# Five groups of blocks by seven products, woven over all steps of a feed-forward part, with wider splits

## The chip, the core and the metric

The kernel runs on one core of a Trainium2 chip. The metric is the device time of one execution in microseconds. Five engines work side by side, each through its own queue of instructions in a fixed order: TensorE (PE in the rows; its weight loads are PEld), VectorE (DVE), ScalarE (ACT), GpSimd (POOL) and SyncE (SP, which issues the loads). Data lies in SBUF, matmul results in eight banks of PSUM.

## What is computed

One decoder layer on 256 tokens in fp32, width 2048: a half-weighted SwiGLU, a mixer (gated linear recurrence and short convolution), a second half-weighted SwiGLU, a gated per-layer input, and a final norm. Cut to what matters here:

```
def swiglu(x, w_gate, w_up, w_down):
    return (jax.nn.silu(x @ w_gate) * (x @ w_up)) @ w_down

h = h + 0.5 * swiglu(rms_norm(h, norm_ffn1), ffn1_gate, ffn1_up, ffn1_down)
u = rms_norm(h, norm_mix); proj = u @ w_in
...                                            # mixer, added to h
h = h + 0.5 * swiglu(rms_norm(h, norm_ffn2), ffn2_gate, ffn2_up, ffn2_down)
h = h + sigmoid(rms_norm(h, norm_ple) @ w_ple_gate) * (p @ w_ple)
y = rms_norm(h, norm_final)
```

Gate and up are 2048 x 5632, that is 44 blocks of 128 columns; down is 5632 x 2048.

## The kernel before

**Splits.** Precision comes from writing each fp32 number as a high and a low part. The unit of work is a step: one weight tile (`raw`, 128 x 16 blocks x 128, 1 MB) is loaded by SP; ACT copies it to the high part (`hi`, L97), DVE subtracts to get the low part (`lo`, L98), and PE forms the product of the 16 blocks with the activations `xs` (high and low side by side, 512 columns): per block one matmul of 512 columns with `hi` (L120) and one of 256 with `lo` (L119, L122), all into one PSUM bank `ps`. A step of 12 or 8 blocks works alike. Before, `hi` and `lo` are half tiles of 8 blocks (four buffers each), so a step has two copies and two subtractions.

**The feed-forward part** goes in chunks of 8, 12, 12 and 12 blocks of the 44: gate and up steps for the chunk (gate: product, scale by the row norm `rb` L153, sigmoid, multiply L375; up: scale, multiply L381, split to `hid` L162 and L163), then 16 down steps, one for each block of the model's width, which multiply `hid` by 8 or 12 blocks and add half the result to `hT` (ACT L206, DVE L207, then L208 which frees the bank).

**Seven products.** In each chunk of 12 the first four blocks of gate and up are a group computed another way: blocks are paired to 2 x 2 (two halves of the tokens, two halves of the 2048 inputs, and gate and up as columns) and seven products of sums take the place of eight. A group has eight parts kp. Each has a half a (three products, nine matmuls of 512 columns, L293 to L295) and a half b (four products, twelve matmuls). The weights come as `sraw`; the sums are `st` (L320 to L322, the last written back into `sraw`); ACT copies and DVE subtracts (L309, L310) give `ahi`, `alo`, `bhi`, `blo`, one buffer each. The activations' sums `xf` are made once per feed-forward part by `forms`, sent to memory by POOL and loaded again for each kp. A group keeps seven of the eight banks from its first matmul to its last. Then `epi` combines them on DVE, and `turn` transposes the result by PE (L392) into `hid`. Before, the halves of a group stand one after each gate or up step of their chunk; the down steps have none.

**Order.** `steps` is one list. Step i loads step i + 3, splits step i + 2, and multiplies itself; a scheduler then places the instructions on each engine by when it expects them to be ready, and that order is fixed.

Of the kernel before, what the change touches and what calls it, by code (L numbers as in the profile page):

```python
# [7 lines left out]
F32 = mybir.dt.float32  # L8
# [24 lines left out]
CHUNKS = ((8, 0), (12, 4), (12, 4), (12, 4))  # L33
NS = 4
NK2 = NB // 2

RAW_BUFS = 3
LOAD_AHEAD = 3
# [13 lines left out]
def kernel(  # L52
# [26 lines left out]
    def tt(shape=(P, T), dtype=F32, tag="t", bufs=6):  # L79
        return tmp.tile(list(shape), dtype, tag=tag, name=tag, bufs=bufs)  # L80
# [13 lines left out]
    def split_piece(s, a, b):  # L94
        hi, lo = s.parts[a // s.half]
        r, sl = s.raw[:, a:b, :], slice(a % s.half, a % s.half + b - a)
        A.activation(hi[:, sl, :], r, AF.Copy)  # L97
        V.tensor_tensor(lo[:, sl, :], r, hi[:, sl, :].bitcast(F32), ALU.subtract)  # L98
# [31 lines left out]
    def weights(s, k):  # L130
        hi, lo = s.parts[k // s.half]
        return hi[:, k % s.half, :], lo[:, k % s.half, :]
# [23 lines left out]
    def sig(src):  # L156
        s = tt(tag="s", bufs=3)
        A.activation(s, src, AF.Sigmoid)
        return s
# [63 lines left out]
    def at(i, f):  # L223
        steps[i].hooks.append(f)
# [17 lines left out]
    FA, FB = ("P1", "P2", "P6"), ("P5", "P3", "P7", "P4")  # L242
    FORMS = {"P4": 0, "P5": 1, "P6": 2, "P7": 3, "P3": 4}
# [9 lines left out]
    def forms(kp, c_gain, sd):  # L253
        pool = st["spool"]
        a = pool.tile([P, 5, P], F32, tag="ec", name="fa", bufs=2)
        f = pool.tile([P, 5, P], F32, tag="ey", name="ff", bufs=2)
# [5 lines left out]
        a11, a21, a12 = a[:, 0, :], a[:, 1, :], a[:, 2, :]  # L262
        V.tensor_tensor(a21, a21, rho, ALU.mult)
        V.tensor_tensor(f[:, 0, :], a[:, 3, :], rho, ALU.mult)
        V.tensor_tensor(f[:, 1, :], a21, f[:, 0, :], ALU.subtract)
        V.tensor_tensor(f[:, 2, :], f[:, 1, :], a11, ALU.subtract)
        V.tensor_tensor(f[:, 3, :], a11, a21, ALU.subtract)
        V.tensor_tensor(f[:, 4, :], a12, f[:, 2, :], ALU.add)
        A.activation(x[:, 0], f, AF.Copy)
        V.tensor_tensor(x[:, 1], f, x[:, 0].bitcast(F32), ALU.subtract)  # L270
        nc.gpsimd.dma_start(sd[:, kp, :], x.rearrange("p a f t -> p (a f t)").bitcast(F32))

    def seven(ws, sd, finish):
# [24 lines left out]
        def ld(kp):  # L298
            def f(s):
                pool = st["spool"]  # L300
                r = g["raw", kp] = pool.tile([P, 4, T2], F32, tag="sraw", name="sraw", bufs=1)
                nc.sync.dma_start(r, ws[kp])
                x = g["xf", kp] = pool.tile([P, 10 * P], F32, tag="xf", name="xf", bufs=2)
                nc.sync.dma_start(x, sd[:, kp, :])
            return f

        def pieces(hi, lo, todo):
            for sl, src in todo:
                A.activation(hi[:, sl, :], src, AF.Copy)  # L309
                V.tensor_tensor(lo[:, sl, :], src, hi[:, sl, :].bitcast(F32), ALU.subtract)  # L310

        def sp_a(kp):
            def f(s):
                pool, r = st["spool"], g["raw", kp]
                t = g["t", kp] = pool.tile([P, 3, T2], F32, tag="st", name="st", bufs=1)
                hi, lo = g["a", kp] = tuple(pool.tile([P, 3, T2], F32R, tag="a" + n, name="a" + n, bufs=1)
                                            for n in ("hi", "lo"))
                pieces(hi, lo, [(slice(0, 2), r[:, 0:2, :])])

                V.tensor_tensor(t[:, 0:2, :], r[:, 0:3:2, :], r[:, 3:4, :].broadcast_to([P, 2, T2]), ALU.add)  # L320
                V.tensor_tensor(t[:, 2, :], t[:, 0, :], r[:, 2, :], ALU.add)
                V.tensor_tensor(r[:, 3, :], t[:, 2, :], r[:, 1, :], ALU.add)  # L322
                pieces(hi, lo, [(2, t[:, 2, :])])
            return f

        def sp_b(kp):
            def f(s):
                pool, r, t = st["spool"], g["raw", kp], g["t", kp]
                hi, lo = g["b", kp] = tuple(pool.tile([P, 4, T2], F32R, tag="b" + n, name="b" + n, bufs=1)
                                            for n in ("hi", "lo"))  # L330

                pieces(hi, lo, [(slice(0, 3, 2), t[:, 0:2, :]), (slice(1, 4, 2), r[:, 2:4, :])])
            return f

        def epi(s):
            pool = st["spool"]

            def e(tag, bufs=2):
                return pool.tile([P, 5 * P], F32, tag=tag, name=tag, bufs=bufs)[:, :T2]

            def silu_mul(c, u):
                y = e("ey")
# [4 lines left out]
            a, c0, v = e("ea", 1), e("ec"), e("ey")  # L347
# [7 lines left out]
            c1 = e("ec")  # L355
# [11 lines left out]
        return res  # L367

    def ffn(wg, wu, wsd, wd, c_gain, c_next, name):
# [15 lines left out]
        def turn(k0, c):  # L385

            for k in range(0, NS, 2):
                ps = new_ps()
                for i in range(2):
                    for w in range(2):  # L390
                        o = i * T + w * P
                        TE.transpose(ps[:, o:o + P], c[w][:, (k + i) * P:(k + i + 1) * P], ident)  # L392
                d = st["hid"][:, k0 + k:k0 + k + 2, :]
                p = ps.rearrange("p (k t) -> p k t", k=2)
                A.activation(d[:, :, :T], p, AF.Copy)
                V.tensor_tensor(d[:, :, T:], p, d[:, :, :T].bitcast(F32), ALU.subtract)

        i0 = len(steps)
        f0 = ng = 0
        for ci, (nf, ns) in enumerate(CHUNKS):  # L400
            last = ci == len(CHUNKS) - 1
            std = []
            for k in range(ns, nf):
                std.append(Step(wg[f0 + k], NB, *gemm_in(g_epi)))
                std.append(Step(wu[f0 + k], NB, *gemm_in(u_epi(k))))
            if ns:
                got = []
                h = seven(wsd[ng], sd, lambda *c, got=got: got.extend(c))
                ng += 1
                seq, std = [*h[:2]], std  # L410
                for x in h[2:]:
                    seq += [std.pop(0), x]
                seq += std
                seq[-1].hooks.append(lambda got=got: turn(0, got))
                steps.extend(seq)
            else:
                steps.extend(std)
            order = [*range(ns, nf), *range(ns)]
            for j in range(NB):
# [11 lines left out]
                add(wd[j][:, f0:f0 + nf, :], nf, mm, epi)  # L431
            f0 += nf
        at(i0 + 5, rows)
# [16 lines left out]
    def mixer():  # L450
# [31 lines left out]
        def i_mm(kc):  # L482
            def mm(s):
                if kc == 0:
                    st["iv"] = new_ps(), new_ps()
                for k in range(4):
                    hi, lo = (t[:, 4 * (k % 2):4 * (k % 2) + 4, :].rearrange("p a c -> p (a c)")
                              for t in s.parts[k // 2])
# [165 lines left out]
        def norm_rows(key, g):  # L654
            d = m["m1"].tile([P, T], F32R, tag="nr", name="nr", bufs=4)
# [276 lines left out]
    n = len(steps)  # L932
    for i, s in enumerate(steps):
        if 0 < i < n - LOAD_AHEAD:
            load(steps[i + LOAD_AHEAD])
# [105 lines left out]
```

## Time and profile before

| | us |
|---|---|
| median of 3 runs (2029.29 to 2030.66) | 2030.2 |
| profiled execution | 2028.77 |
| its span | 2027.0 |
| PE busy (99% of the span) | 2002.1 |
| PE's weight loads busy (85%) | 1731.7 |
| DVE busy (81%) | 1636.0 |
| ACT busy (55%) | 1117.1 |

The profile's span runs from the first instruction to the last; the execution around it is 1.8 us longer. The first feed-forward part lies at 0 to 741 us, the mixer to 1181, the second feed-forward part to 1909, the per-layer input after it. An engine's busy time says how much work it has; whether a wait matters is seen only from what the engine that ends last, PE here, was waiting for in that stretch. The rows below show both for the stretches that the change touches.

### The profile page before, as it was taken

The numbers are of one execution on the slowest core, as the hardware profiler recorded it, in microseconds if no ns is written. First come the engines' busy times: TensorE is split into PE (matmuls) and PEld (weight loads), VectorE is DVE, ScalarE is ACT, GpSimd is POOL, SyncE is SP. The second block draws the span as 40 slices with busy tenths as digits, with TensorE's granted clock in tenths as the row PEclk, the third lists the DMA queues.
The fourth block names the chain that finished last, engine by engine and source line by source line (L and its number), as shares of the span: only waits on it lengthen the run. The fifth ranks groups of instructions, "written<-read, shape, count | busy, mean of one in ns | idle before, by whom it ended". The sixth has DMA issues, their size and how long they took to land.

```text
span 2027.0 us, 28859 instructions
## 1 busy us (share of the span) xinstructions
PE 2002.1 (99%) x11094; PEld 1731.7 (85%) x11094; DVE 1636.0 (81%) x2645; ACT 1117.1 (55%) x1716; POOL 11.6 (1%) x23
## 2 busy tenths in 40 slices
PE   8999999999999999999999999999999999999997
PEld 7888888888888888888888888888888888888886
DVE  8988886888688775689798789788968886887886
ACT  7655555555555554553566556455555555555663
POOL 0000000000000000000000000000000000000000
PEclk9999999999999999999999999999999999999998
DMA  8686666665665465544355567766666666654742
GB/s 293 211 277 242 233 205 216 219 237 200 222 232 198 156 212 187 189 166 146 129 184 187 187 227 274 226 232 226 208 208 224 232 202 220 228 202 153 249 164 84
DMA packets 69546, 419.93 MB, mean 207 GB/s; under 512 B 7712, under 2 KB 7968, under 8 KB 35744
## 3 DMA queue, kind: packets, MB, share of 16 engines
q1 hardware_dynamic: 67104, 407.60, 59.0%
q0 software_dynamic: 2304, 10.49, 1.3%
q8 instruction: 87, 1.43, 0.3%
q14 instruction: 51, 0.42, 0.1%
HBM read 405.48 MB, written 12.58 MB: 206 GB/s over the span
## 4 chain that ended last, share of the span: by engine, by line
PE 89%; DVE 4%; DMA 4%; issue 1%; ACT 1%; SPq 0%; DVEq 0%; ACTq 0%
PE ps L120 49%; PE ps L119 23%; PE ps L294 3%; PE ps L295 3%; PE ps L293 3%; PE ps L122 2%; DVE lo L98 2%; DMA sraw<-w1s 1%; DMA raw<-w1d 1%; DMA raw<-w1u 1%; PE ps L591 1%; PE ps L494 1%; PE ps L493 1%; PE ps L492 1%; DMA sraw<-w2s 1%
## 5 line engine op out<-in xcount | busy, mean ns | idle before, releaser
L120 PE MATMUL ps<-xs,hi 128*128 128x512 f32 x3056 | 1082.8, 395 | 9.5 <-DVE xs L167 6.1
L98 DVE TENSOR_TENSOR lo<-raw,hi 128x1024 fp32r<-128x1024 f32 (+2 forms) x660 | 751.1, 1139 | 239.3 <-ACT hi L97 235.7
L97 ACT ACTIVATE hi<-raw 128x1024 fp32r<-128x1024 f32 (+2 forms) x660 | 652.7, 990 | 516.6 <-PE ps L120 323.6
L119 PE MATMUL ps<-xs,lo 128*128 128x256 f32 x2865 | 801.5, 280 | 0.4 <-DVE lo L98 0.2
L120 PEld LDWEIGHTS ps<-xs,hi 128*128 128x128 f32 x3056 | 569.7, 188 | 137.5 <-ACT hi L97 7.2
L119 PEld LDWEIGHTS ps<-xs,lo 128*128 128x128 f32 x2865 | 538.0, 188 | 10.4 <-DVE lo L98 1.8
L120 PE MATMUL ps<-hid,hi 128*128 128x512 f32 x1384 | 477.6, 394 | 0.0
L119 PE MATMUL ps<-hid,lo 128*128 128x256 f32 x1258 | 354.4, 283 | 0.5 <-ACT hid L162 0.5
L120 PEld LDWEIGHTS ps<-hid,hi 128*128 128x128 f32 x1384 | 251.5, 188 | 48.8
L119 PEld LDWEIGHTS ps<-hid,lo 128*128 128x128 f32 x1258 | 236.2, 188 | 7.3 <-ACT hid L162 1.3
L309 ACT ACTIVATE ahi<-sraw 128x1024 fp32r<-128x1024 f32 x48 | 51.0, 1063 | 125.2 <-DMA sraw<-w1s 61.5
L146 ACT ACTIVATE t<-ps 128x256 f32<-128x256 f32 x191 | 70.2, 372 | 88.3 <-PE ps L120 88.3
L320 DVE TENSOR_TENSOR st<-sraw 128x1024 f32<-128x1024 f32 x48 | 58.8, 1224 | 69.2 <-DMA sraw<-w1s 38.7
L147 DVE TENSOR_TENSOR t<-ps,t 128x256 f32<-128x256 f32 x191 | 80.3, 421 | 24.0 <-ACT t L146 23.9
L120 PE MATMUL ps<-mixout,hi 128*128 128x512 f32 x240 | 83.6, 397 | 0.0
L153 DVE TENSOR_TENSOR t<-t,rb 128x256 f32<-128x256 f32 x183 | 76.9, 422 | 2.7
L293 PE MATMUL ps<-bhi,xf 128*128 128x512 f32 x192 | 74.9, 390 | 0.0
L295 PE MATMUL ps<-blo,xf 128*128 128x512 f32 x192 | 74.9, 390 | 0.0
L294 PE MATMUL ps<-bhi,xf 128*128 128x512 f32 x192 | 74.9, 390 | 0.0
L208 DVE SCALAR_TENSOR_TENSOR hT<-ps,t 128x256 f32<-128x256 f32 x141 | 59.7, 424 | 13.7 <-DVE t L207 1.4
L207 DVE TENSOR_TENSOR t<-hT,t 128x256 f32<-128x256 f32 x141 | 59.1, 420 | 10.6 <-ACT t L206 10.6
L206 ACT ACTIVATE t<-ps 128x256 f32<-128x256 f32 x141 | 51.9, 369 | 27.5 <-PE ps L120 27.5
(234 smaller groups left out, 2078.7 us busy)
## 6 DMA issues: line engine op xcount, KB each, us to landing
raw<-w_in SPq DMA_DIRECT2D x48, 1024.0 KB, 4.8
raw<-w1d SPq DMA_DIRECT2D x48, 768.0 KB, 4.2
raw<-w2d SPq DMA_DIRECT2D x48, 768.0 KB, 4.3
raw<-w2g SPq DMA_DIRECT2D x32, 1024.0 KB, 4.9
raw<-w2u SPq DMA_DIRECT2D x32, 1024.0 KB, 5.1
raw<-w1u SPq DMA_DIRECT2D x31, 1024.0 KB, 5.3
raw<-w1g SPq DMA_DIRECT2D x30, 1024.0 KB, 5.0
xf<-forms SPq DMA_DIRECT2D x48, 640.0 KB, 4.0
```

The source lines that it names most:

```text
L97: A.activation(hi[:, sl, :], r, AF.Copy)
L98: V.tensor_tensor(lo[:, sl, :], r, hi[:, sl, :].bitcast(F32), ALU.subtract)
L119: TE.matmul(ps[:, T:], lo, m[:, :T], start=False, stop=False)
L120: TE.matmul(ps, hi, m, start=first, stop=last)
L146: A.activation(t, ps[:, T:], AF.Copy)
L147: V.tensor_tensor(t, ps[:, :T], t, ALU.add)
L153: V.tensor_tensor(dst, t, rb, ALU.mult)
L207: V.tensor_tensor(t, hT[:, j, :], t, ALU.add)
L208: V.scalar_tensor_tensor(hT[:, j, :], ps[:, :T], c, t, ALU.mult, ALU.add)
L293: TE.matmul(g[p], x_lo, hi[:, i, :], start=kp == 0, stop=False)
L294: TE.matmul(g[p], x_hi, hi[:, i, :], start=False, stop=False)
L295: TE.matmul(g[p], x_hi, lo[:, i, :], start=False, stop=kp == NK2 - 1)
```

## The change

- `CHUNKS` now names groups per chunk: 0, 1, 2 and 2, five for each feed-forward part in place of three. 20 of 44 blocks go by seven products, 12 before.
- `weave` orders a feed-forward part: after 14 gate and up steps, half steps of the groups, in one stream, stand after the other steps in the ratio of 4/3 per full step, down steps included; half steps left over at a chunk's end follow at once. A group's transposes are steps of their own, at least two steps after its end. No half step stands within 1.5 steps after a group's end.
- `hi` and `lo` of a step are whole tiles in two buffers. ACT still copies in two halves, DVE subtracts once.
- Half a is split in one operation on each engine (1536 columns), half b in one of 2048. All four sums are in `st`, and `raw` buffers, four of them, serve both kinds of steps; loads run four steps ahead.
- `forms` makes four sums, and the fifth is taken as it is. Some buffers of small tiles are fewer.

```diff
-CHUNKS = ((8, 0), (12, 4), (12, 4), (12, 4))
+CHUNKS = ((8, 0), (12, 1), (12, 2), (12, 2))
+LEAD = 14
+HALVES = 4 / 3
-RAW_BUFS = 3
-LOAD_AHEAD = 3
+RAW_BUFS = 4
+LOAD_AHEAD = 4
...
     def new_parts(s):
-        s.half = s.nk // 2 if s.nk > 8 else s.nk
-        s.parts = [tuple(wpool.tile([P, NB // 2, P], F32R, tag=t, name=t) for t in ("hi", "lo"))
-                   for _ in range(s.nk // s.half)]
+        s.parts = tuple(wpool.tile([P, NB, P], F32R, tag=t, name=t, bufs=2) for t in ("hi", "lo"))
...
         new_parts(s)
-        for k0 in range(0, s.nk, s.half):
-            split_piece(s, k0, k0 + s.half)
+        hi, lo = s.parts
+        h = s.nk // 2
+        for a in (0, h):
+            A.activation(hi[:, a:a + h, :], s.raw[:, a:a + h, :], AF.Copy)
+        V.tensor_tensor(lo[:, :s.nk, :], s.raw[:, :s.nk, :], hi[:, :s.nk, :].bitcast(F32), ALU.subtract)
...
+        def parts(key, kp, n, src):
+            hi, lo = g[key, kp] = tuple(st["spool"].tile([P, n, T2], F32R, tag=key + t, name=key + t, bufs=1)
+                                        for t in ("hi", "lo"))
+            A.activation(hi, src, AF.Copy)
+            V.tensor_tensor(lo, src, hi.bitcast(F32), ALU.subtract)
...
+                r = g["raw", kp]
+                parts("a", kp, 3, r[:, 0:3, :])
+                t = g["t", kp] = st["spool"].tile([P, 4, T2], F32, tag="st", name="st", bufs=1)
                 V.tensor_tensor(t[:, 0:2, :], r[:, 0:3:2, :], r[:, 3:4, :].broadcast_to([P, 2, T2]), ALU.add)
                 V.tensor_tensor(t[:, 2, :], t[:, 0, :], r[:, 2, :], ALU.add)
-                V.tensor_tensor(r[:, 3, :], t[:, 2, :], r[:, 1, :], ALU.add)
-                pieces(hi, lo, [(2, t[:, 2, :])])
+                V.tensor_tensor(t[:, 3, :], t[:, 2, :], r[:, 1, :], ALU.add)
...
         def sp_b(kp):
-            def f(s):
-                pool, r, t = st["spool"], g["raw", kp], g["t", kp]
-                hi, lo = g["b", kp] = tuple(pool.tile([P, 4, T2], F32R, tag="b" + n, name="b" + n, bufs=1)
-                                            for n in ("hi", "lo"))
-
-                pieces(hi, lo, [(slice(0, 3, 2), t[:, 0:2, :]), (slice(1, 4, 2), r[:, 2:4, :])])
-            return f
+            return lambda s: parts("b", kp, 4, g["t", kp])
...
+        def other(x, ci):
+            w = x.nk / NB
+            steps.append(x)
+            state["n"] += 1
+            state["rest"] -= w
+            for t in turns:
+                t[1] += w
+            if state["n"] < LEAD:
+                return
+            state["credit"] += w * HALVES
+            while halves and state["credit"] >= 1 and state["rest"] <= 0:
+                half()
+                state["credit"] -= 1
+            state["credit"] = min(state["credit"], 2.0)
+            if ci is not None:
+                turn_all(ci, 2.0)
+
+        for ci, (std, down) in enumerate(others):
+            for x in std:
+                other(x, ci)
+            while halves and groups[halves[0][0]][2] <= ci:
+                half()
+            turn_all(ci, 0.0)
+            for x in down:
+                other(x, None)
```

The order of the instructions shows what this does on the engines. In the new kernel the lines are L117 for `lo`, L315 for `alo` and `blo`, L322 to L324 for `st`, L210 and L211 for a down step's sum, L122, L123 and L125 for its matmuls.

DVE where half steps stood in the kernel before, between gate and up steps:

```order
L321 TENSOR_TENSOR st_3861<-st_3861,sraw_3807 128x512
L98 TENSOR_TENSOR lo_3884<-raw_3859,hi_3883 128x1024
L147 TENSOR_TENSOR t_3852<-ps_3819,t_3852 128x256
L322 TENSOR_TENSOR sraw_3807<-st_3861,sraw_3807 128x512
L153 TENSOR_TENSOR t_3852<-t_3852,rb_76 128x256
L310 TENSOR_TENSOR alo_3863<-st_3861,ahi_3862 128x512
L381 TENSOR_TENSOR t_3852<-t_3852,t_3783 128x256
L98 TENSOR_TENSOR lo_3886<-raw_3859,hi_3885 128x1024
L163 TENSOR_TENSOR hid_303<-t_3852,hid_303 128x256
L310 TENSOR_TENSOR blo_3934<-st_3861,bhi_3933 128x2x512
L310 TENSOR_TENSOR blo_3934<-sraw_3807,bhi_3933 128x2x512
```

DVE in the down steps of chunk 1 in the new kernel, the queue of one down step with one kp:

```order
L210 TENSOR_TENSOR t_3206<-hT_69,t_3206 128x256
L117 TENSOR_TENSOR lo_3233<-raw_3174,hi_3232 128x1536
L211 SCALAR_TENSOR_TENSOR hT_69<-ps_3181,t_3206 128x256
L315 TENSOR_TENSOR alo_3320<-raw_3266,ahi_3319 128x1536
L322 TENSOR_TENSOR st_3323<-raw_3266 128x1024
L323 TENSOR_TENSOR st_3323<-st_3323,raw_3266 128x512
L324 TENSOR_TENSOR st_3323<-st_3323,raw_3266 128x512
L315 TENSOR_TENSOR blo_3380<-st_3323,bhi_3379 128x2048
```

The halves have moved beside down steps; between the last sum (L324) and `blo`, which needs the high parts made from that sum, other work stood before and none stands now.

DVE in the down steps of chunk 0, before (`ps_1181`, `ps_1208` are two of them):

```order
L207 TENSOR_TENSOR t_1198<-hT_69,t_1198 128x256
L207 TENSOR_TENSOR t_1225<-hT_69,t_1225 128x256
L208 SCALAR_TENSOR_TENSOR hT_69<-ps_1181,t_1198 128x256
L208 SCALAR_TENSOR_TENSOR hT_69<-ps_1208,t_1225 128x256
L98 TENSOR_TENSOR lo_1232<-raw_1202,hi_1231 128x1024
```

and in the new kernel (`ps_1575` and `ps_1623` are neighbours there):

```order
L210 TENSOR_TENSOR t_1592<-hT_69,t_1592 128x256
L211 SCALAR_TENSOR_TENSOR hT_69<-ps_1575,t_1592 128x256
L117 TENSOR_TENSOR lo_1619<-raw_1568,hi_1618 128x1024
L322 TENSOR_TENSOR st_1723<-raw_1660 128x1024
L323 TENSOR_TENSOR st_1723<-st_1723,raw_1660 128x512
L210 TENSOR_TENSOR t_1640<-hT_69,t_1640 128x256
L315 TENSOR_TENSOR alo_1720<-raw_1660,ahi_1719 128x1536
L211 SCALAR_TENSOR_TENSOR hT_69<-ps_1623,t_1640 128x256
L117 TENSOR_TENSOR lo_1647<-raw_1596,hi_1646 128x1024
L324 TENSOR_TENSOR st_1723<-st_1723,raw_1660 128x512
L315 TENSOR_TENSOR blo_1786<-st_1723,bhi_1785 128x2048
```

A group's work now stands among the down steps' sums, `alo` behind L210 of the second down step.

PE at the border of those two down steps in the new kernel, behind a half b:

```order
L299 MATMUL ps_1063<-blo_1665,xf_1541 128x512
L299 MATMUL ps_1064<-blo_1665,xf_1541 128x512
L123 MATMUL ps_1575<-hid_293,hi_1525 128x512
L125 MATMUL ps_1575<-hid_293,lo_1526 128x256
L122 MATMUL ps_1575<-hid_293,lo_1526 128x256
...
L122 MATMUL ps_1575<-hid_293,lo_1526 128x256
L123 MATMUL ps_1575<-hid_293,hi_1525 128x512
L123 MATMUL ps_1623<-hid_293,hi_1570 128x512
L125 MATMUL ps_1623<-hid_293,lo_1571 128x256
```

The two down steps stand together, while the group whose products are `ps_1063` and `ps_1064` holds its seven banks; before, no group was open there.

## Rows read from the trace of the kernel before

**Rows 1.** The page's parts 1 and 4: busy time, and the chain by engine.

```profile
PE 2002.1 (99%) x11094; PEld 1731.7 (85%) x11094; DVE 1636.0 (81%) x2645; ACT 1117.1 (55%) x1716; POOL 11.6 (1%) x23
PE 89%; DVE 4%; DMA 4%; issue 1%; ACT 1%; SPq 0%; DVEq 0%; ACTq 0%
```

**Rows 2.** Busy time by stretch: chunk 0's downs, woven gate/up, chunk 1's downs, mixer.

```profile
core 0: us, PE busy (x) PEld busy (x) DVE busy (x) ACT busy (x) POOL busy (x), PEclk, DMA share, GB/s
103.40:149.00 45.60, 45.15 (x258) 39.25 (x257) 35.57 (x57) 22.45 (x36) 0.53 (x1) 1.00 0.86 292
149.00:266.70 117.70, 117.52 (x617) 99.89 (x616) 101.00 (x134) 66.80 (x90) 0.00 (x0) 1.00 0.67 232
278.80:346.30 67.50, 67.50 (x386) 59.11 (x385) 47.31 (x73) 32.60 (x51) 0.00 (x0) 1.00 0.63 204
910.40:932.60 22.20, 22.20 (x131) 19.97 (x130) 21.76 (x49) 9.49 (x13) 0.00 (x0) 1.00 0.44 150
```

**Rows 3.** Timeline of PE: start, duration, line; first matmuls of steps and the transposes.

```profile
277.96 1.04 PE L392 MATMUL ps<-cst,ec 128*128 128x128 f32 x8
278.75 0.48 PE L120 MATMUL ps<-hid,hi 128*128 128x512 f32 x1
...
397.40 0.40 PE L293 MATMUL ps<-bhi,xf 128*128 128x512 f32 x1
...
400.14 0.40 PE L120 MATMUL ps<-xs,hi 128*128 128x512 f32 x1
...
405.75 0.39 PE L293 MATMUL ps<-ahi,xs 128*128 128x512 f32 x1
...
407.84 0.40 PE L120 MATMUL ps<-xs,hi 128*128 128x512 f32 x1
...
413.46 0.40 PE L293 MATMUL ps<-bhi,xf 128*128 128x512 f32 x1
```

**Rows 4.** Timeline of DVE in the same stretch, operations queued one behind another.

```profile
418.73 0.42 DVE L163 TENSOR_TENSOR hid<-t,hid 128x256 fp32r<-128x256 f32 x1
419.07 1.22 DVE L310 TENSOR_TENSOR blo<-st,bhi 128x1024 fp32r<-128x1024 f32 x1
420.20 1.22 DVE L310 TENSOR_TENSOR blo<-sraw,bhi 128x1024 fp32r<-128x1024 f32 x1
421.34 1.22 DVE L98 TENSOR_TENSOR lo<-raw,hi 128x1024 fp32r<-128x1024 f32 x1
422.48 0.42 DVE L147 TENSOR_TENSOR t<-ps,t 128x256 f32<-128x256 f32 x1
422.93 0.42 DVE L153 TENSOR_TENSOR t<-t,rb 128x256 f32<-128x256 f32 x1
```

**Rows 5.** Timeline, all engines: emptying a bank after PE's step ended at 405.75.

```profile
405.95 0.38 ACT L146 ACTIVATE t<-ps 128x256 f32<-128x256 f32 x1 [1.69 <-PE ps L120]
...
406.37 0.42 DVE L147 TENSOR_TENSOR t<-ps,t 128x256 f32<-128x256 f32 x1 [0.80 <-ACT t L146]
```

**Rows 6.** Groups of instructions by line and shape: busy us, mean ns; idle before.

```profile
L98 DVE TENSOR_TENSOR lo<-raw,hi 128x1024 fp32r<-128x1024 f32 x460 | 562.2, 1223 | 144.6 <-ACT hi L97 141.4
L97 ACT ACTIVATE hi<-raw 128x1024 fp32r<-128x1024 f32 x460 | 486.0, 1057 | 326.6 <-PE ps L120 172.5 <-issue 87.5 <-PE ps L494 20.8
...
L206 ACT ACTIVATE t<-ps 128x256 f32<-128x256 f32 x141 | 51.9, 369 | 27.5 <-PE ps L120 27.5
...
L309 ACT ACTIVATE ahi<-st 128x512 fp32r<-128x512 f32 x48 | 30.2, 629 | 30.3 <-DVE st L321 30.3
```

**Rows 7.** Waits, whole span: us in total, times, longest us.

```profile
ACT hi L97 <- PE ps L120: 323.6, 274, 4.3
DVE lo L98 <- ACT hi L97: 235.7, 283, 3.2
...
PE ps L120 <- DVE xs L167: 6.1, 2, 5.8
```

**Rows 8.** The page's part 6: a load's issues, size, median us to landing.

```profile
raw<-w_in SPq DMA_DIRECT2D x48, 1024.0 KB, 4.8
```

More of the change, by code (lines that the diff above doesn't have):

```diff
@@ L94, in split_piece @@
     def split_piece(s, a, b):
[L95 to L98, printed above, removed]
+        hi, lo = (t[:, a:b, :] for t in s.parts)
+        r = s.raw[:, a:b, :]
+        A.activation(hi, r, AF.Copy)
+        V.tensor_tensor(lo, r, hi.bitcast(F32), ALU.subtract)
     def load(s, n=1):
@@ L367, in seven, with weave, half, turn_all @@
         return res
+    def weave(groups, others):
+        halves = [(gi, x) for gi, (h, _, _) in enumerate(groups) for x in h]
+        turns = []
+        state = {"n": 0, "credit": 0.0, "rest": 0.0}
+        def half():
+            gi, x = halves.pop(0)
+            steps.append(x)
+            if x.epi:
+                turns.append([gi, 0.0])
+                state["rest"] = 1.5
+        def turn_all(ci, least):
+            for t in [t for t in turns if groups[t[0]][2] == ci and t[1] >= least]:
+                turns.remove(t)
+                for x in groups[t[0]][1]:
+                    steps.append(x)
+                    if halves and state["rest"] <= 0:
+                        half()
+                        state["credit"] -= 1
+        def other(x, ci):
+            w = x.nk / NB
+            steps.append(x)
+            state["n"] += 1
[7 more added lines that the diff above has]
+                half()
+                state["credit"] -= 1
+            state["credit"] = min(state["credit"], 2.0)
[5 more added lines that the diff above has]
+            while halves and groups[halves[0][0]][2] <= ci:
+                half()
+            turn_all(ci, 0.0)
+            for x in down:
+                other(x, None)
     def ffn(wg, wu, wsd, wd, c_gain, c_next, name):
@@ L398, in ffn @@
+            return [step(k) for k in range(0, NS, 2)]
         i0 = len(steps)
-        f0 = ng = 0
-        for ci, (nf, ns) in enumerate(CHUNKS):
+        groups = []
+        others = []
+        f0 = 0
+        for ci, (nf, ng) in enumerate(CHUNKS):
             last = ci == len(CHUNKS) - 1
-            std = []
-            for k in range(ns, nf):
+            for i in range(ng):
+                got = []
+                h = seven(wsd[len(groups)], sd, lambda *c, got=got: got.extend(c))
+                groups.append((h, turn(i * NS, got), ci))
+            std, down = [], []
+            for k in range(ng * NS, nf):
@@ L418, in ffn @@
-            order = [*range(ns, nf), *range(ns)]
+            order = [*range(ng * NS, nf), *range(ng * NS)]
             for j in range(NB):
@@ L430, in epi @@
                         partial(s.ps, j, 0.5)
-                add(wd[j][:, f0:f0 + nf, :], nf, mm, epi)
+                down.append(Step(wd[j][:, f0:f0 + nf, :], nf, mm, epi))
+            others.append((std, down))
             f0 += nf
+        weave(groups, others)
         at(i0 + 5, rows)
@@ L932 @@
     n = len(steps)
+    loaded = 4
     for i, s in enumerate(steps):
-        if 0 < i < n - LOAD_AHEAD:
-            load(steps[i + LOAD_AHEAD])
+        while i > 0 and loaded < min(n, i + LOAD_AHEAD + 1):
+            load(steps[loaded])
+            loaded += 1
         if 1 < i < n - SPLIT_AHEAD:
@@ L1007, in sevens @@
         res, f0 = [], 0
-        for nf, ns in CHUNKS:
-            if ns:
-                g, u = (w[:, f0 * P:(f0 + NS) * P].reshape(NK2, 2, P, NS * P) for w in (gate, up))
+        for nf, ng in CHUNKS:
+            for i in range(ng):
+                c = slice((f0 + i * NS) * P, (f0 + (i + 1) * NS) * P)
+                g, u = (w[:, c].reshape(NK2, 2, P, NS * P) for w in (gate, up))
                 res.append(np.stack([g[:, 0], g[:, 1], u[:, 1], u[:, 0]], 2))
```

102 lines of the change are left out of this document (43 added, 59 removed).

## Prediction

> **What bounds the kernel now.** I read the page's busy times first. TensorE (PE) works 2002 of 2027 us and PE lines make up 89% of the chain that ended last [rows 1], so every matmul removed is time gained, as long as nothing makes PE wait. Its longest waits are single ones of some 6 us [rows 7]. Next I read the stretches, because a change that adds VectorE (DVE) work must be judged where that work lands. In the stretch that already mixes half steps of a seven-product group with gate and up steps, DVE is busy 101 of 117.7 us and PE still stands only 0.2 us. In a stretch of nothing but 12-block down steps DVE has 47.3 of 67.5, and in one part of the mixer 21.8 of 22.2 [rows 2]. So DVE is the second bound, near everywhere and close in places. Last I read the waits of DVE and ACT: DVE's low parts wait 236 us in all for ACT's high parts, ACT's high parts 324 us for PE to release their tiles [rows 7]. That idle time is hidden today because both run ahead of PE. What runs ahead, and by how much, is what the change touches.
>
> **PE's own work.** From the starts of a step's first matmul and of its successor's [rows 3]: half b 400.14 - 397.40 = 2.74 us, a gate or up step 405.75 - 400.14 = 5.61 (the next one 5.62), half a 407.84 - 405.75 = 2.09. One kp (half a and half b) is 4.83. Eight transposes take 278.75 - 277.96 = 0.79. Sixteen down steps of 12 blocks fill 67.5 us, 4.22 each; those of 8 blocks 45.6, 2.85 each [rows 2]. Over both FFNs four groups more are formed by seven products. Each takes away 8 gate and up steps and brings 8 kp and 8 transposes: -32 x 5.615 = -179.7, +32 x 4.83 = +154.6, +4 x 0.79 = +3.2, together **-21.9 us**. The matmul forms are those of the rows, so the bounds are close: -19 to -24.
>
> **DVE's work.** Starts of queued operations [rows 4] give 1.135 us for 1024 columns (419.07 to 420.20 to 421.34), 0.34 for 256 that wait for nothing (418.73 to 419.07), 0.45 for 256 that need the one ahead (422.48 to 422.93). The line through 0.34 and 1.135 gives 0.605 for 512 columns, 1.67 for 1536 and 2.2 for 2048. No row shows 1536 or 2048; twice 1.135 is their upper end, so a joined operation saves 0.07 at most. ACT takes 0.63 for 512 and 1.06 for 1024 [rows 6], by the same line 1.48 for 1536 and 1.9 for 2048. A kp then costs DVE 1.67 + 1.135 + 2 x 0.605 + 2.2 = 6.2. Thirty-two kp more are +198, four epilogues +29 (7 x 0.605 + 4 x 0.75), 32 gate and up steps less -118 (2.27 for the low part and 1.42 for the rest: 0.34 + 0.45 + 0.45 for a gate, 0.34 more for an up), some 240 joined operations -17: DVE goes from 1636 to about 1728 us, 86% of the shorter time. As a total that still fits.
>
> **The added waits.** They come from order within a queue, so I walked the new order of DVE and PE with these durations, stretch by stretch.
>
> (1) Down steps of chunks 1 and 2. In the first five of each, a whole kp stands beside every down step. PE needs 4.83 + 4.22 = 9.05 us. DVE's row per period (shown with the change) is L210 0.45, lo 1.67, L211 0.34, alo 1.67, st 1.135 + 0.605 + 0.605, then blo 2.2. But bhi now takes all four columns of st in one ACT operation and blo stands next in the queue: DVE waits 0.08 (two hops of 0.04, 406.33 to 406.37 [rows 5]) + 1.9. Sum 10.65, or 1.6 more than PE, with single buffers for ahi, alo, bhi and blo, so that no lead builds up. Four such stretches of five: **+32**. Lower end 17, if each stretch first uses up a lead of one down step's 4.2 us less 0.5.
>
> (2) Down steps of chunk 0. Seven of eight PSUM banks are held, so of two neighbouring down steps the second waits until the first is emptied: 0.2 from PE's end to ACT's start (405.75 to 405.95 [rows 5]), 0.37 ACT [rows 6], 0.45 and 0.45 on DVE, some 0.1 back: 1.6. Then alo of half a is queued behind L210 of the down step that PE has just ended: 0.2 + 0.37 + 0.45 + 1.67 + 0.1, less 0.46 of matmuls that need only ahi: 2.3. Half b, which waits for bhi and blo as in (1), comes 1.4 late. That is 5.3 for three down steps and two halves, three times per FFN: **+32**. If alo were early, 5 would be left per FFN, 10 in all.
>
> (3) In chunk 2 two to three kp of one group run with hardly a gate or up step between, and the transposes and epilogue fall there. DVE needs 6.2 + 1.98 = 8.2 per kp against 4.83; over a bit more than two kp 7.5 per FFN: **+15**.
>
> (4) Elsewhere a kp stands beside 1.5 gate and up steps: DVE 8.2 + 1.5 x 3.62 = 13.6 against PE's 4.83 + 8.42 = 13.25, 0.35 over, in some 22 kp per FFN, with the ends of groups about 11 per FFN: **+22** (from 0, since a lead can hide 0.35, to 44).
>
> (5) The last 12-block down steps have no half steps. The chain of a step, from PE's release over two ACT copies of 768 to one lo of 1536 and two more operations on both engines, is 4.6 against 4.22; part of it overlaps: **+2.4** in all.
>
> (6) The other stretches without half steps (mixer, output projection, last layer) lose lead too: whole tiles in two buffers give one step of lead where four half tiles gave one and a half. From PE's release 0.15 + 2 x 1.06 + 2.2 = 4.5 of 5.61 us, so 1.1 is left and I price it at **0**. The cover is that slack; where DVE has other work in the way, as in the mixer stretch of 98% [rows 2], it is gone (third rival).
>
> Loads: a woven down period needs 0.79 + 1.05 + 0.66 MB in 9.05 us, 275 GB/s; 292 was moved in one stretch of before [rows 2], a 1 MB load lands after 4.8 us [rows 8] and is now asked for four steps ahead. I take 0, with (1)'s own delay as the cover. The forms' edits and the shared raw buffers I also put at 0.
>
> Joining bhi is one operation against two. The rows give the joined form 0.07 us per operation, and DVE waits 1.98 for it where a half-wide copy would have been ready after 1.06. The Trainium skill says the same of both sides (Perfetto Trace Analysis, Optimizing Scalar/DVE Operations): larger operations help a saturated engine, while breaking them up lets work complete sooner if an unsaturated Scalar or Vector engine holds up others. By it, ACT at 55% should not be given the wide copy; two pieces would take 0.85 off each of the 20 periods of (1), 17 us. The sum goes by the order as it stands.
>
> Waits: 32 + 32 + 15 + 22 + 2.4 = 103.4. With PE's -21.9 that is +81.5. The profiled execution of 2028.8 becomes 2110.3; the median of the runs lies 1.4 above it, so **2112**.
>
> On the banks behind (2) the Trainium skill states that independent matmul groups should rotate through PSUM banks so that emptying one overlaps the next (Perfetto Trace Analysis, Matmuls). With seven banks held no rotation is left; the trace of before shows no such pair, so its 1.6 us is not measured here.
>
> **Rivals.**
> (A) Everything stays hidden: 2030.2 - 21.9 = **2008**. For it: in the mixed stretch of before DVE is at 86% with similar chains, and PE does not wait [rows 2]; the scheduler also puts the lo matmuls of a half step last, where lateness costs least. Against it: in that stretch blo did not wait for a copy of the whole st, and two half tiles each had their own release.
> (B) A quarter to two fifths of the waits appear, 18 to 42 us: **2026 to 2050**. It needs the lower ends of (1) and (2) together and nothing from (4).
> (C) The shorter lead also shows in pure steps: 0.5 us in each of some 148 of them, 74 more: **2186**. It decides where DVE has over 1.1 us of other work ahead of a lo. For it: the mixer at 98%. Against it: most pure stretches leave DVE a quarter free.
> The other side of my forecast is (A): it holds if less than 22 of the 103 us come up.
>
> **Chances and range.** Forecast case (2050 to 2155) 0.66, (A) 0.16, (B) 0.09, of which 0.04 lies within 0.2% (some 4 us, about what a measurement of this kernel can tell from no change), (C) 0.09. Faster 0.16, same 0.04, slower 0.80. Eight in ten needs part of (A) and of (C): 2008 to 2165. The forecast's own range is 2050 to 2155: every term at its low end (17 + 10 + 5 + 0 + 0 less 21.9) would even be 2040, and (4) at 44 with (1) at 2.1 per period 2144.
>
> **What would show it.** In the profile after: PE busy near 1980 us in a span of about 2109. In woven down stretches periods of 10.6 us and blo (L315) waiting near 2 us for bhi (L314), PE waiting for blo or bhi (L299, L297). In chunk 0, PE's L123 waiting 1.6 us for L211, and L299 over 2 us for alo. In the mixer and the last layer no new PE wait. The prediction is wrong if PE's idle time stays near 25 us (A), or if L122 and L123 wait for lo in pure stretches (C).

## The result and the profile after

| | before | after |
|---|---|---|
| median, us | 2029.7 (2029.1 to 2030.7) | 2158.9 (2156.6 to 2165.8) |
| span of the profiled execution, us | 2027.0 | 2157.3 |

The changed kernel takes 1.064 times the time of the one before (95% interval 1.062 to 1.067): 129 us more, against 82 forecast. The time lies in the wide range of the prediction (2008 to 2165), near its upper end, and 4 us above the range of the forecast case itself (2050 to 2155).

The page's busy times and its chain by engine, after (before: [rows 1]):

```profile
PE 2028.3 (94%) x10774; PEld 1700.9 (79%) x10774; DVE 1726.2 (80%) x2307; ACT 1112.1 (52%) x1624; POOL 11.6 (1%) x23
...
PE 29%; DVE 6%; ACT 3%; issue 2%; DMA 2%; DVEq 0%; ACTq 0%; SPq 0%
```

DVE has 1726 us, where 1728 were summed up. PE now stands idle 129 us where it stood 25. The chain could be followed back only to 1260 us, so its shares add up to 42%; in what it covers PE lines make up 69%, against 89% of the whole before, with DVE at 14% and ACT at 7%. PE's busy time has risen although it has less work: a matmul counts as busy until its modelled end, also when the next one is late, and at half clock one of 512 columns is shown with 0.63 us in place of 0.39. So the busy figure is not PE's work here.

What PE waited for, whole span (us in total, times, longest us), after:

```profile
PE ps L297 <- ACT bhi L314: 17.5, 18, 2.1
PE ps L125 <- DVE lo L117: 16.9, 12, 3.3
PE ps L297 <- ACT ahi L314: 14.5, 16, 1.3
PE ps L123 <- DVE hT L211: 14.3, 13, 1.6
PE ps L123 <- ACT hi L116: 14.2, 13, 1.6
PE ps L299 <- DVE alo L315: 10.9, 10, 3.2
...
PE ps L437 <- DVE hid L443: 4.7, 4, 1.7
PE ps L299 <- DVE blo L315: 3.8, 18, 0.2
```

Three of these are the forecast's own: L297 waiting for `bhi`, L299 for `alo`, and L123 for L211, the held banks. Three are not: L297 waiting for `ahi`, and L125 for `lo` and L123 for `hi`, which are a step waiting for its own split; the forecast had put that at nothing outside the last down steps.

Busy time by stretch, after (columns as in [rows 2]): first chunk's gate and up steps, its down steps, chunk 1's down steps, chunk 2's gate and up steps, the last down steps, the mixer, the last layer:

```profile
0.00:123.90 123.90, 106.40 (x549) 89.29 (x550) 102.17 (x209) 76.34 (x143) 4.59 (x12) 0.96 0.68 239
123.90:217.40 93.50, 79.17 (x382) 60.88 (x382) 70.24 (x78) 44.92 (x62) 0.00 (x0) 1.00 0.65 224
...
366.20:480.40 114.20, 107.21 (x544) 87.76 (x544) 94.10 (x95) 54.87 (x63) 0.00 (x0) 1.00 0.66 234
480.40:569.40 89.00, 81.33 (x405) 65.79 (x404) 71.73 (x72) 44.90 (x50) 0.00 (x0) 0.98 0.60 214
...
737.50:810.10 72.60, 70.37 (x397) 59.61 (x396) 51.25 (x75) 40.74 (x77) 0.00 (x0) 0.98 0.56 186
810.10:1257.90 447.80, 442.11 (x2489) 384.36 (x2488) 335.06 (x540) 220.05 (x355) 2.74 (x3) 1.00 0.49 170
...
2039.30:2157.30 118.00, 104.55 (x606) 90.77 (x604) 88.28 (x160) 63.09 (x125) 0.00 (x0) 0.94 0.40 145
```

The mixer of the kernel before, for comparison:

```profile
741.30:1181.30 440.00, 439.81 (x2488) 384.12 (x2487) 339.82 (x612) 228.24 (x357) 2.73 (x3) 1.00 0.51 174
```

The mixer, which the weave does not touch, is 7.8 us longer with the same matmuls. The first stretch has a granted clock of 0.96 where it was 1.00.

To hold the forecast's terms against the trace I took, for every matmul, the time from its start to the next one's, less what its shape takes undisturbed: 0.2345 us for 512 columns and 0.117 for 256 (sixteen of each are 5.62 us, [rows 3]). What is over is waiting; what is over at a granted clock of 0.5 is put under clock.

| us | forecast | before | after |
|---|---|---|---|
| (1) down steps of chunks 1 and 2 | 32 | 0 | 38.8 |
| (2) down steps of chunk 0 | 32 | 0.9 | 29.9 |
| (3) gate and up steps of chunk 2 | 15 | 2.7 | 21.7 |
| (4) gate and up steps of chunks 1 and 3 | 22 | 1.5 | 21.8 |
| (5) last down steps | 2.4 | 0.2 | 8.3 |
| (6) first chunk's gate and up steps, mixer, last layer | 0 | 12.4 | 36.5 |
| half clock, but for the last 15 us of both | 0 | 0 | 11 |
| PE's work (what is left of the 130.3 between the spans) | -21.9 | | -20 |

### The profile page after: what moved, and what is told of

Same layout as the page of the kernel before. It is cut to its first block, busy times and chain, and to the rows that moved or that the text cites. A ratio compares the mean times of both kernels' runs of the same rounds, so it can differ in the third digit from the quotient of the medians.

```text
span 2157.3 us, 27835 instructions
## 1 busy us (share of the span) xinstructions
PE 2028.3 (94%) x10774; PEld 1700.9 (79%) x10774; DVE 1726.2 (80%) x2307; ACT 1112.1 (52%) x1624; POOL 11.6 (1%) x23
## 5 line engine op out<-in xcount | busy, mean ns | idle before, releaser
L123 PE MATMUL ps<-xs,hi 128*128 128x512 f32 x2544 | 905.5, 397 | 18.4 <-ACT hi L97 6.5
L117 DVE TENSOR_TENSOR lo<-raw,hi 128x2048 fp32r<-128x2048 f32 (+2 forms) x310 | 624.0, 2013 | 129.2 <-ACT hi L116 127.4
L122 PE MATMUL ps<-xs,lo 128*128 128x256 f32 x2385 | 670.1, 281 | 0.0
L123 PEld LDWEIGHTS ps<-xs,hi 128*128 128x128 f32 x2544 | 476.5, 189 | 126.2 <-ACT hi L116 7.0
L123 PE MATMUL ps<-hid,hi 128*128 128x512 f32 x1384 | 494.5, 397 | 23.5 <-DVE hT L211 14.3
L122 PEld LDWEIGHTS ps<-xs,lo 128*128 128x128 f32 x2385 | 450.8, 189 | 8.1 <-DVE lo L98 1.2
L122 PE MATMUL ps<-hid,lo 128*128 128x256 f32 x1258 | 355.3, 283 | 0.6 <-ACT hid L165 0.6
L123 PEld LDWEIGHTS ps<-hid,hi 128*128 128x128 f32 x1384 | 257.5, 188 | 91.0 <-issue 23.7
L315 DVE TENSOR_TENSOR blo<-st,bhi 128x2048 fp32r<-128x2048 f32 x80 | 183.2, 2290 | 76.4 <-ACT bhi L314 75.8
L122 PEld LDWEIGHTS ps<-hid,lo 128*128 128x128 f32 x1258 | 237.2, 189 | 6.0 <-ACT hid L165 1.3
L314 ACT ACTIVATE bhi<-st 128x2048 fp32r<-128x2048 f32 x80 | 153.0, 1912 | 129.7 <-DVE st L324 80.1
L314 ACT ACTIVATE ahi<-raw 128x1536 fp32r<-128x1536 f32 x80 | 118.6, 1483 | 63.7 <-DMA raw<-w1s 27.9
L297 PE MATMUL ps<-bhi,xf 128*128 128x512 f32 x320 | 129.1, 403 | 17.6 <-ACT bhi L314 17.5
L315 DVE TENSOR_TENSOR alo<-raw,ahi 128x1536 fp32r<-128x1536 f32 x80 | 140.1, 1751 | 4.5 <-ACT ahi L314 4.3
L298 PE MATMUL ps<-bhi,xf 128*128 128x512 f32 x320 | 126.6, 396 | 0.0
L299 PE MATMUL ps<-blo,xf 128*128 128x512 f32 x320 | 110.5, 401 | 4.0 <-DVE blo L315 3.8
L322 DVE TENSOR_TENSOR st<-raw 128x1024 f32<-128x1024 f32 x80 | 97.6, 1220 | 16.0 <-DMA raw<-w1s 7.9
L210 DVE TENSOR_TENSOR t<-hT,t 128x256 f32<-128x256 f32 x141 | 59.2, 420 | 48.6 <-ACT t L209 48.4
L297 PEld LDWEIGHTS ps<-bhi,xf 128*128 128x128 f32 x320 | 60.8, 190 | 38.0 <-ACT bhi L314 27.0
```

The costliest lines, as they stand in the source:

```text
L117: V.tensor_tensor(lo[:, :s.nk, :], s.raw[:, :s.nk, :], hi[:, :s.nk, :].bitcast(F32), ALU.subtract)
L122: TE.matmul(ps[:, T:], lo, m[:, :T], start=False, stop=False)
L123: TE.matmul(ps, hi, m, start=first, stop=last)
L210: V.tensor_tensor(t, hT[:, j, :], t, ALU.add)
L297: TE.matmul(g[p], x_lo, hi[:, i, :], start=kp == 0, stop=False)
L298: TE.matmul(g[p], x_hi, hi[:, i, :], start=False, stop=False)
```

## Experiments

My theory after the result was that the added waits come from what is joined (a step's split and half b) and from where half steps stand. Rivals were one of the two alone, and the mere number of groups. The scheduler places the instructions of every kernel anew, so what an edit is worth below includes the order that came with it. For the first run PE's order hardly changes (97% of its matmuls are of the same kind and shape at the same place); in the others it changes more.

**Wider splits alone.** The kernel before with this edit, which joins the tiles and the subtraction, and nothing else of the change:

```diff
-        s.half = s.nk // 2 if s.nk > 8 else s.nk
-        s.parts = [tuple(wpool.tile([P, NB // 2, P], F32R, tag=t, name=t) for t in ("hi", "lo"))
-                   for _ in range(s.nk // s.half)]
+        s.parts = tuple(wpool.tile([P, NB, P], F32R, tag=t, name=t, bufs=2) for t in ("hi", "lo"))
...
-        for k0 in range(0, s.nk, s.half):
-            split_piece(s, k0, k0 + s.half)
+        hi, lo = s.parts
+        h = s.nk // 2
+        for a in (0, h):
+            A.activation(hi[:, a:a + h, :], s.raw[:, a:a + h, :], AF.Copy)
+        V.tensor_tensor(lo[:, :s.nk, :], s.raw[:, :s.nk, :], hi[:, :s.nk, :].bitcast(F32), ALU.subtract)
```

> The kernel before with one edit: hi and lo of a step are whole tiles in two buffers, and DVE subtracts once per step (L117 of the new kernel). Groups, order and seven-product splits stay. Theory (waits come from what is joined and from where half steps stand, and the joining of a step's own split costs lead only where DVE is full): PE's added waits at the start, in the first chunk's gate and up steps and in the mixer were 36 us in the new kernel against 13 of before, so +15 to +25 us, about 2050. Rival 1 (the wide splits are the main loss): over +60, above 2090. Rival 2 (the loss comes from half steps beside down steps alone): within 4 us of before.

Measured 2064.5, ratio 1.018 (1.015 to 1.021): +36, more than the theory said and less than the first rival. Its chunk 1 down steps and its mixer:

```profile
287.20:357.60 70.40, 68.25 (x384) 58.59 (x384) 46.33 (x58) 30.75 (x51) 0.00 (x0) 1.00 0.60 201
757.40:1206.50 449.10, 443.39 (x2489) 385.53 (x2488) 334.69 (x540) 220.01 (x355) 2.74 (x3) 1.00 0.50 170
```

and what its PE waited for:

```profile
PE ps L123 <- DVE lo L115: 8.4, 11, 2.9
PE ps L121 <- ACT hi L114: 8.1, 10, 1.0
```

Sixteen down steps take 70.4 us in place of 67.5 [rows 2], with DVE at 46 of 70 us: DVE and ACT are not full there, the chain of one step is too long. The mixer takes 449 us, as in the changed kernel, here with as many buffers of small tiles as before. The wide split of a step therefore costs by itself, in stretches that have no half steps, and step (6) of the forecast is wrong.

**Half tiles back in the new kernel** (the same edit undone there):

> The new kernel with one edit undone: hi and lo of a step are again half tiles in four buffers, two subtractions per step. Theory: the waits of pure stretches go (L125 for lo, some 20 us) and about 6 us of clock with them, while those of the woven stretches stay: about 2133 (2125 to 2145). Rival 1 (wide splits are the main loss): under 2090. Rival 2 (only the half steps beside down steps matter): 2155 or more, as more DVE operations fill the woven stretches.

Measured 2079.8: 79 us less, where the theory had 26. Rival 1 called it. Half tiles also matter where half steps stand: the waits in stretches (1) to (4) fall from 112 to 49 us.

**What the half tiles undo.** Whole tiles kept, two subtractions:

```diff
         for a in (0, h):
-            A.activation(hi[:, a:a + h, :], s.raw[:, a:a + h, :], AF.Copy)
-        V.tensor_tensor(lo[:, :s.nk, :], s.raw[:, :s.nk, :], hi[:, :s.nk, :].bitcast(F32), ALU.subtract)
+            split_piece(s, a, a + h)
```

> The new kernel, whole tiles in two buffers kept, but each step's low part made in two DVE subtractions, each behind its own ACT copy. It tells apart what half tiles (79 us less) undo. Theory (the width of the subtraction: DVE may not begin before both copies, and PE may not begin before the whole): most of it, 40 to 70 us less, about 2105. Rival (the buffers: a whole tile is released only at a step's end, so that ACT's copies, and what is queued behind them, come late): under 20 us less, above 2139.

Measured 2139.8, 19 us less: the theory fell, the rival's figure came true. So of the 79 us some 19 go with the width of the subtraction and the other 60 with the buffers: the same bytes of SBUF, as four half tiles or as two whole ones. One thing more differs between the two runs: the steps of 8 blocks are split in two here, and in one piece with half tiles. The stretches with those steps hold some 15 of the 60 us. PE's waits with two subtractions on whole tiles:

```profile
PE ps L296 <- ACT ahi L313: 19.3, 18, 5.3
PE ps L122 <- ACT hi L97: 17.9, 10, 6.0
```

and on half tiles:

```profile
PE ps L122 <- ACT hi L99: 6.2, 1, 6.2
...
PE ps L296 <- ACT ahi L313: 4.6, 2, 4.3
```

One wait of 6 us stands at the kernel's start in all of them. The others were for ACT's copies. A whole tile is released when PE has done the last block of a step, so the copies for the step after next cannot begin earlier, and `ahi` or `bhi`, queued behind them on ACT, come late too. That the queue passes the delay on is what the waits suggest; no run changed ACT's order alone.

**Half b in two pieces** in the new kernel:

```diff
-            return lambda s: parts("b", kp, 4, g["t", kp])
...
+                for sl in (slice(0, 2), slice(2, 4)):
+                    A.activation(hi[:, sl, :], t[:, sl, :], AF.Copy)
+                    V.tensor_tensor(lo[:, sl, :], t[:, sl, :], hi[:, sl, :].bitcast(F32), ALU.subtract)
```

> The new kernel with half b split in two pieces, bhi and blo of two sums each, in place of one operation of 2048 columns. Theory (in woven stretches DVE stands idle for bhi): the wait of blo for bhi, 76 us of DVE time, nearly goes, and periods of woven down steps fall from 11.0 to about 9.3 us: 25 to 45 us less, about 2125. Rival (DVE's amount of work or the held banks set the period): under 8 us less, above 2150.

Measured 2100.4, 58 us less: more than expected, and the rival is out. DVE's wait for bhi:

```profile
DVE blo L334 <- ACT bhi L333: 2.2, 4, 1.0
```

It was 75.8 us (47 times) in the new kernel.

**Both edits:**

> The new kernel with both edits of before: half tiles for steps (79 us less alone) and half b in two pieces (58 us less alone). Added they would give 2022, below the kernel before. Theory (both edits remove the same thing, the time in which DVE stands idle in its queue behind one wide copy; what is left are held banks and bursts at the ends of chunks): 2060 (2045 to 2075). Rival (two separate causes that add): under 2035.

Measured 2056.8. The two gains, 79 and 58, overlap to 102 together, as the theory said.

**Fewer groups:**

```diff
-CHUNKS = ((8, 0), (12, 1), (12, 2), (12, 2))
+CHUNKS = ((8, 0), (12, 1), (12, 1), (12, 1))
```

> The new kernel with three groups per feed-forward part, one in each chunk of 12, all else as changed. PE's work is 21.9 us more than with five. Theory (waits come with the half steps that stand beside down steps and in dense bursts, about 115 us of them with 80 kp): with 48 kp three fifths of them or less, 115 - 70 + 21.9: about 2110 (2090 to 2130). Rival 1 (joined operations alone, whatever the number of groups): 2140 or more. Rival 2 (the number of groups is all): within 15 us of before, since the count is that of before.

Measured 2139.4, 20 us less; the theory fell by 29 us. Waits went from 157 to 117 us, a quarter less, where two fifths were expected. In the first chunk of the first feed-forward part (37 us against 35) and in the mixer (12 in both) they do not depend on the number of groups: the weave still starts in the first chunk, and the step's split is as wide. With 12 blocks as before, but woven and wide, the kernel is 110 us slower than before. So the number of groups is not the cause. Rival 1, joined operations whatever the number, had 2140 or more and missed by under 1 us; the later start below shows that place counts beside them.

**No low parts:**

```diff
-        V.tensor_tensor(lo[:, :s.nk, :], s.raw[:, :s.nk, :], hi[:, :s.nk, :].bitcast(F32), ALU.subtract)
...
-        return hi[:, k, :], lo[:, k, :]
+        return hi[:, k, :], hi[:, k, :]
...
+            g[key, kp] = hi, hi
...
-            V.tensor_tensor(lo, src, hi.bitcast(F32), ALU.subtract)
```

> The new kernel without the DVE subtractions that make the low parts of steps and sevens; PE reads the high parts in their place, with the same matmuls in number and shape. Left out: the low parts of most weights. Theory (PE's work is 21.9 us less and the added waits are DVE's queue and what waits for it): 2008 plus the waits for held banks, some 20 pairs of down steps at 1.6, about 2035 (2010 to 2050). Rival (PE's work is not less, or ACT and banks set the time): over 2080.

Measured 2012.8, ratio 0.992 (0.989 to 0.995). Its busy times:

```profile
PE 1983.9 (99%) x10774; PEld 1699.7 (85%) x10774; DVE 852.6 (42%) x1837; ACT 1125.9 (56%) x1624; POOL 11.6 (1%) x23
```

The PE work is there to be had: 1984 us busy at 99%, 18 less than before, with the same list of steps and the same loads. The waits for banks that I expected to remain (some 27 us) were mostly absent: L122 waited 3.2 us for L210. But the order of PE is another one. While a group is open, two down steps follow each other 15 times in the new kernel, and seven of these pairs wait 1.55 us each; here part of a half step stands between any two. So this run does not show what a held bank costs, and what the missing subtractions gave cannot be told from what the order gave.

**Place alone**, in two settings (wide operations, and both edits of above): one half step after each other step whatever its size, from the end of the first chunk's gate and up steps on.

```diff
-LEAD = 14
+LEAD = 16
...
-            state["credit"] += w * HALVES
+            state["credit"] += 1.0
```

> The new kernel with its wide operations, and only the weave changed: one half step after each other step, from the end of the first chunk's gate and up steps on. Theory (joined operations are the larger part, place the smaller): 10 to 30 us less, about 2138. Rival (place is the main cause): under 2100.

> As the kernel of half tiles and pieces, and the weave places one half step after each other step whatever its size, from the end of the first chunk's gate and up steps on (LEAD 16, credit 1.0 per step). Eighty halves then meet eighty other steps, and PE has a half between nearly any two down steps. Theory (what is left of the waits is place: first chunk, held banks, bursts): 25 us less than without it, about 2035 (2020 to 2055). Rival (place does not matter once the pieces are small): within 8 us of it.

Measured 2174.6 with wide operations (16 more than the new kernel) and 2071.4 with small ones (15 more than without this weave). Both expectations fell. An even spread over steps is not an even spread over time: beside an 8-block down step of 2.85 us a half step brings DVE to 1.14 + 0.79 + 3.1 = 5.0 of 5.3 us. This sum, made afterwards, is an argument and not a measurement.

**Later start.** On top of both edits half steps begin after the first chunk's down steps, and stand closer, since fewer steps are left for them:

```diff
-LEAD = 14
-HALVES = 4 / 3
+LEAD = 32
+HALVES = 1.5
```

> Half tiles and pieces (2057), and the weave begins after the first chunk's down steps (LEAD 32) with 1.5 half steps per full step. In the kernel with half tiles and pieces the first chunk's four stretches hold 31 of PE's 61 us of waits and all of the slow clock. Theory (those waits come from half steps on top of the forms and of the short down steps): 20 to 35 us less, about 2030, level with before. Rival (the waits move with the half steps to where they are put now): within 8 us of 2057 or above.

Measured 2017.6 (2015.0 to 2021.0), ratio 0.993 (0.991 to 0.995): 12 us less than the kernel before, and 39 less than with the early start, a little over the theory's 20 to 35. Its first rows of the page, and PE's waits:

```profile
PE 1987.8 (98%) x10774; PEld 1703.2 (84%) x10774; DVE 1745.1 (86%) x2665; ACT 1146.5 (57%) x1672; POOL 11.6 (1%) x23
```

```profile
PE ps L122 <- ACT hi L99: 6.5, 1, 6.5
PE ps L122 <- DVE hT L210: 4.4, 5, 2.3
```

DVE is at 86% of the span, more than in the slow kernel, and PE hardly waits: 29 us by the sum above, 18 in the kernel before. The woven down steps of chunk 1:

```profile
295.70:406.10 110.40, 110.40 (x570) 93.21 (x569) 104.11 (x127) 63.69 (x76) 0.00 (x0) 1.00 0.73 260
```

DVE 104 of 110 us, and PE without a gap.

The same later start with the wide operations of the new kernel:

> The new kernel with its wide operations and whole tiles, and only the weave of the fastest kernel: half steps begin after the first chunk's down steps (LEAD 32), 1.5 per full step. With half tiles and pieces this place took 2057 to 2018. Theory (whole tiles and the joined half b are the larger part and stay as they are wherever the half steps stand): 15 to 45 us less than the new kernel, about 2125 (2110 to 2145). Rival (place is the main cause, and the small operations only help where half steps stand badly): under 2080.

Measured 2098.9, 60 us less than the new kernel, between theory and rival. With the two edits as one axis and the start as the other:

| us | early start | late start |
|---|---|---|
| wide splits, half b in one | 2158.9 | 2098.9 |
| half tiles, half b in two | 2056.8 | 2017.6 |

The small operations are worth 102 or 81 us, the place (start and ratio together) 60 or 39.

**Four groups**, late start, small operations:

> As the one that begins late, with four groups per feed-forward part (one, one and two in the chunks of 12) and 1.1 half steps per full step. PE's work is 10 us more than with five groups and 10 less than before; DVE stays near 82% in woven stretches. Theory (waits grow with how full DVE is where the half steps stand): 15 us of waits above before's at most, 2020 to 2035. Rival (any half step beside down steps costs): 2045 or more.

Measured 2054.0 (2046.3 to 2055.1). The theory that waits follow how full DVE is falls here: less work for DVE, and 36 us slower than with five groups. The rival had the number, but not the reason: with five groups more half steps stand beside down steps, and PE hardly waits. About 10 us are PE's work. Some 20 lie in the down steps of chunk 2 alone, waits for `ahi` and behind them six stretches of half clock, 3.4 us each:

```profile
PE ps L296 <- ACT ahi L313: 13.2, 6, 2.3
```

In this kernel ACT waited 33 us for weights of half a to land, 22 with five groups, but which load was late and why was not tried.

## Why the prediction was right, and where it was off

**PE's work**, -21.9: right. The span's difference leaves -20, and the kernel without low parts shows it by itself.

**Term (1)**, 1.6 us per period: right in mechanism and nearly in size. DVE's timeline in the down steps of chunk 1, after (start, duration):

```profile
389.61 2.29 DVE L315 TENSOR_TENSOR blo<-st,bhi 128x2048 fp32r<-128x2048 f32 x1 [2.06 <-ACT bhi L314]
391.81 0.42 DVE L210 TENSOR_TENSOR t<-hT,t 128x256 f32<-128x256 f32 x1
392.15 1.75 DVE L117 TENSOR_TENSOR lo<-raw,hi 128x1536 fp32r<-128x1536 f32 x1
393.82 0.42 DVE L211 SCALAR_TENSOR_TENSOR hT<-ps,t 128x256 f32<-128x256 f32 x1
394.15 1.75 DVE L315 TENSOR_TENSOR alo<-raw,ahi 128x1536 fp32r<-128x1536 f32 x1
395.82 1.22 DVE L322 TENSOR_TENSOR st<-raw 128x1024 f32<-128x1024 f32 x1
397.07 0.69 DVE L323 TENSOR_TENSOR st<-st,raw 128x512 f32<-128x512 f32 x1
397.80 0.69 DVE L324 TENSOR_TENSOR st<-st,raw 128x512 f32<-128x512 f32 x1
400.55 2.29 DVE L315 TENSOR_TENSOR blo<-st,bhi 128x2048 fp32r<-128x2048 f32 x1 [2.06 <-ACT bhi L314]
```

It is the predicted row, in order. The period is 10.94 us against 10.65, blo waits 2.06 for bhi against 1.98, and 1536 columns start 1.67 apart as interpolated. PE needs 9.05 and has to wait. Not every one of the twenty periods waits, as each stretch begins with some lead; in return pairs of down steps with held banks occur here too, which the term had left out: four of them, some 7 of the 38.8 us. Such a pair, ACT, DVE and PE:

```profile
420.75 0.38 ACT L209 ACTIVATE t<-ps 128x256 f32<-128x256 f32 x1 [7.55 <-PE ps L123]
...
421.17 0.42 DVE L210 TENSOR_TENSOR t<-hT,t 128x256 f32<-128x256 f32 x1 [5.04 <-ACT t L209]
421.69 0.42 DVE L211 SCALAR_TENSOR_TENSOR hT<-ps,t 128x256 f32<-128x256 f32 x1
...
422.27 0.47 PE L123 MATMUL ps<-hid,hi 128*128 128x512 f32 x1 [1.55 <-DVE hT L211]
```

1.55 us, 1.6 forecast. DVE had stood idle 5.04 us until ACT's copy came, so the wait is the emptying itself and not DVE's lateness. The Trainium skill's rule that breaking up instructions lets work complete sooner (Perfetto Trace Analysis, Optimizing Scalar/DVE Operations) agrees with the run in two pieces, 58 us less. The 17 worked out by it for the periods of (1) were too few: there alone the waits fell by 31 us, and by about as much in (2) to (4) together.

**Terms (2) and (4)**, 32 and 22 against 29.9 and 21.8: right in sum. Inside (2) the single waits were smaller than walked (alo 1.2 us at three of five places of the first part, 2.3 forecast) and more of them. **(3)**, 15 against 21.7, was low by a third. **(5)**, 2.4 against 8.3, and **(6)**, 0 against 24 more than before, are the terms that were mis-sized. The step that failed is "From PE's release 0.15 + 2 x 1.06 + 2.2 = 4.5 of 5.61 us, so 1.1 is left and I price it at 0". It counted one step with DVE and ACT free at once. Where the chain is near the step's length, as in a 12-block down step, or where DVE holds other work, the slack is gone: 70.4 for 67.5 us, and 449 for 440 in the mixer of the kernel with wider splits alone. Of the 24 us of (6) about 13 also come with wider splits alone, 8 of them in the mixer; the rest lies in the first chunk's gate and up steps, with 12 of the 16.9 us of L125 for `lo`, where the forms and the first half steps stand too, and was not taken apart. Rival (C) named this with 0.5 us in every pure step, 74 us; it was a third of that, in places. Its sign, steps of pure stretches waiting for `lo`, came up only faintly: 1.6 us in the mixer, where another 4.1 are waits for `nr` and `K`, small tiles that ACT and DVE made late. Rival (B)'s 18 us are a sixth of the 103, not a quarter; its range of 2026 to 2050 hangs on that, the forecast does not.

**The clock** was left out. In the first chunk of the new kernel PE waited 3.2 us for alo and 3.2 for lo. The stretches behind:

```profile
96.00:99.30 3.30, 0.48 (x3) 0.04 (x1) 3.30 (x7) 2.68 (x5) 0.53 (x1) 1.00 0.40 164
99.30:102.70 3.40, 3.06 (x7) 2.48 (x8) 3.40 (x7) 2.29 (x5) 0.00 (x0) 0.50 0.15 57
102.70:106.10 3.40, 0.45 (x2) 0.00 (x0) 3.40 (x5) 3.04 (x4) 0.53 (x1) 1.00 0.58 193
106.10:109.50 3.40, 3.18 (x11) 2.79 (x12) 3.40 (x13) 2.50 (x4) 0.00 (x0) 0.50 0.90 311
```

After a stretch in which PE was busy 0.5 of 3.3 us the granted clock is 0.50 (1.2 in place of 2.4 GHz) for 3.4 us. Matmuls of 512 columns then start 0.43 us apart in place of 0.2345, so by an estimate from these two some 1.5 us are lost, and a wait of 3.2 us costs up to half as much again. Over the span this is 11 us.

**The forms**, put at 0, are not free either: ACT now copies a22 first and waits there for the earlier `xf` to be sent, which the kernel before did not show.

```profile
ACT xf L271 <- DMA forms<-xf: 31.5, 9, 8.0
```

What PE lost by it in the first chunk was not tried by itself.

**The loads**, put at 0, leave a trace too: ACT waited 51 us for the weights of half a, where it waited 113 before. Without low parts the same loads took a span of 2011 us, with 11 us of such waits, so their rate alone does not set the time. What PE lost by these waits was not tried by itself.

**Rival (A)**, everything hidden, was wrong for this kernel. It came nearly true for the same groups with small operations and a later start, at 2017.6 against its 2008.

## What to carry to other kernels

Total busy time did not decide: DVE was at 80% in the slow kernel and at 86% in the fast one. What decided here, by the runs that undo the joining and move the start, was how early a queue's next operation could begin; so read what each wide operation must wait for in whole, and walk the order of the queue for one period. Buffers that are joined are released late: two whole tiles in place of four half tiles cost some 60 us here, where each joined operation saved 0.07. That the late release is the reason is argued from the waits. Before joining operations, see whether their engine waits in its queue: there a saved operation can be worth nothing.

## What the runs showed of the hardware

That short waits are followed by a granted clock of 0.50 for 3.4 us was new to me: it happened seven times in the new kernel (once for 6.8 us) and never in the kernel before, the last 16 us of both left out. When a down step follows another while a group holds seven banks, PE waits 1.55 us, the same at all seven places of the new kernel where it waits. Joined DVE operations cost what the line through smaller ones gives: 1.67 us from start to start for 1536 columns and 2.2 for 2048, so a joined operation saves 0.07 us and no more.
